# The first two tiles of the branch gate ga, projected ahead of the conv branch's output projection

## The chip, the cores and the metric

The kernel runs on one core of one Trainium2 chip, in one launch. The metric is the device time of one execution in microseconds, as the median of several runs.

## The reference, cut to what matters

One layer of a hybrid block over 512 latent tokens of 1024 features, with 256 context tokens ahead. The part around the change merges two branches:

```python
z = h @ w_in            # q, k, v, g, dd, cb, cc, ch, ga, gb are columns of z
y_gla = (o * silu(g)) @ w_gla_out            # o: normed heads of the gated linear attention
u = cc * ch
uc = seq_conv(u)        # width 3, within rows of 64 tokens
y_conv = (cb * uc) @ w_conv_out
merged = sigmoid(ga) * y_gla + sigmoid(gb) * y_conv
x = x + gt1 * (merged @ w_mix_out)
x = x + gt2 * swiglu(modulate(rmsnorm(x)))
```

The six modulation vectors (shift, scale and gate, twice) are `silu(c) @ w_ada + b_ada`.

## The kernel before

Everything is float32, computed as three products of exactly split halves (hi·hi, hi·lo, lo·hi): `mm3` (L148 to L151, all matmuls through L145). A weight comes in units of 512 KB into one of four raw buffers by a DMA from SyncE's queue (`raw_unit`, L118), ScalarE casts the high half `h_*` and VectorE subtracts the low half `l_*` (`split`, both recorded as L103); each half has four buffers. Two units make a slab of 256 columns (`Slab`), and `proj` multiplies it into two tiles of 128 features by 512 tokens: 24 matmuls of 128x512 for a tile, 48 for a pair. The tile accumulates in one of three PSUM banks that `proj` uses in turn (`bank`); the bank is free once the tile is read out.

Names in the rows leave numbers out, so `r_co`, `h_co`, `l_co` are the raw, high and low parts of the slabs of w_conv_out. In the order rows the numbers stand: `co0` is the slab of the first pair, `yc01` the second tile of pair 0.

After the attention the work runs in this order, pair by pair (four pairs of tiles each):

1. The short convolution (loop from L818): projections cc, ch and cb of a pair; VectorE makes `u`, then `uc`, then `cbu` = cb * uc (L845, which reads cb's bank out), and `split` makes `cuh` and `cul`, two of the eight parts of `cu`.
2. The conv branch's output (loop at L849): `yc`, a pair at a time, contracted over all eight parts of `cu`, in order; L854 multiplies the tile into `m` (the sigmoid of gb) and so reads the bank out.
3. The split of the attention's output `og` into `ogh` and `ogl`.
4. The loop at L862: a pair of `ga` tiles, ScalarE's sigmoid into `sa` (L869), then a pair of `yg` tiles, `yg * sa + m` (L876, L877) and the split into `me`.
5. The output projection `mx`, the residual, the second norm and SwiGLU.

Between these pairs `ada_tick` (L775) does the rest of the modulation in 16 steps, one at a call: it closes the last step with a small matmul `ad` of its sums (L781; L783 adds them to `gt`), loads two more units of w_ada (`r_wa`) and has VectorE fold them into `acc` with one operation and seven more (L805, L807), which are then cast and split as `accs`. The convolution loop calls it three times a pair, the loop of `yc` once a pair and the loop of `ga` once a pair, so the last four steps (`acc50` to `acc53`) are opened in the loop of `yc`.

What sets the order: outside the attention a scheduler orders each engine's instructions by when it reckons them ready. VectorE, ScalarE and SyncE's queue run them strictly in that order, so an instruction that waits holds all behind it.

Of the kernel before, what the change touches and what calls it, by code (L numbers as in the profile page):

```python
# [12 lines left out]
AF = mybir.ActivationFunctionType  # L13
# [18 lines left out]

# order of a head's attention on the tensor engine: its parts, and between them steps of other work
ORDER0 = "5 B 7 B 9 B 4 B 14 B 1 F0 5 B 1 kt0 1 A 4 F1 kv0 4 kt1 1 A 1 A 2 kv1 3 A 3 o 8 A 13 ot"
ORDER = "10 B 1 B 2 B 6 B 9 B 4 B F0 17 kt0 F1 A 2 kv0 2 kt1 11 kv1 A A 1 A A 2 o 33 ot"
ORDER3 = "3 B 4 B 3 B 12 B 4 B B 9 F1 F0 11 kt0 5 kv0 2 kt1 11 kv1 13 o 10 ot"

# columns of w_in
CQ, CK, CV, CG, CD = 0, 512, 1024, 2048, 3072
CCB, CCC, CCH, CGA, CGB = 3104, 4128, 5152, 6176, 7200  # L40

# rows of the small-vector tile
R_GM, R_GF, R_BA, R_GH, R_BD, R_WC, R_N = 0, 8, 16, 64, 66, 74, 98
# [3 lines left out]
def hybrid_block(ctx: ExitStack, tc: tile.TileContext, x, c, ctxt, c_ctx, w_ada, b_ada, g_mix, w_in,  # L47
# [45 lines left out]
    def pin(ins):  # L93
        """keeps the order on an engine as written, while a head's attention runs"""
        if pinned[0]:
            tc.keep_in_program_order(ins)
# [16 lines left out]

    # ---- weights: raw rows in, exact split into two parts of the tensor engine's width
    def raw_unit(src, name):
# [12 lines left out]
    class Slab:  # L128
        """Columns of a weight with 1024 rows (or k0..k1 tiles of rows), in units of at most 4 KiB per partition."""

# [24 lines left out]
    def rstd_of(ss, n, width, name):  # L155
        """(ss / width + EPS) ** -0.5 of n columns"""
        r = sm.tile([P, n], F32, tag=f"rs{n}", name=f"rs_{name}")
        act_.activation(r, ss, AF.Sqrt, bias=eps, scale=1.0 / width)
        dve.reciprocal(r, r)
        return r  # L160

    # ---- constants; the conditions first
    c_rows = cst.tile([16, P], F32, name="c_rows")
# [26 lines left out]
    for d in range(2):  # L190
        m = u2(f"m{d}")
        if d == 0:
            nc.vector.memset(m[:, P:2 * P], 1.0)
            nc.vector.tensor_copy(ones, m[:, P:2 * P])
        s = 1 if d == 0 else -1
        nc.gpsimd.memset(m, 1.0)
        # keep where s * (i - j) >= 0
        nc.gpsimd.affine_select(out=m[:, :P], in_=m[:, :P], compare_op=ALU.is_ge, fill=0.0, base=0,
                                pattern=[[s, P]], channel_multiplier=-s)
        mk = cst.tile([P, NT, P], U8, name=f"mask{d}")  # L200
        for s_ in range(NT):
            nc.vector.tensor_copy(mk[:, s_, :], m[:, :P])
        masks.append(mk)
# [10 lines left out]
    c2v = c2.rearrange("p (s k) -> p k s", s=2)  # L214
    # both parts of the conditions as four columns; their sum by pairs
    c4 = cst.tile([P, KT, 4], F32R, name="c4")
# [4 lines left out]

    # ---- small vectors, as columns
    vrow = u2("vrow")
# [11 lines left out]

    # ---- head: norm and transpose of the tokens; shift and scale of the first norm
    hp = tc.alloc_tile_pool(name="hp", bufs=1)
# [54 lines left out]
    def modulate(f):  # L292
        n = 4 if f in ADA_SPLIT else 2
        rsb = sm.tile([4, 256], F32, tag="adar", name=f"adar{f}", bufs=2)
        nc.vector.tensor_copy(rsb[0:n, :], rows[f][0:n, :256])
        cp = gbank(f"adac{f}")
        for s_ in range(2):
            nc.tensor.matmul(cp[:, 2 * s_:2 * s_ + 2], rsb[0:n, s_ * P:(s_ + 1) * P], sel[0:n, :], start=True, stop=True)
        nc.vector.tensor_tensor(modT[:, f], cp[:, 0:4].rearrange("p (s c) -> p s c", s=2),
                                vec[:, R_BA + f:R_BA + f + KT + 1:KT].unsqueeze(2).broadcast_to([P, 2, 2]), ALU.add)  # L300
        # g * (1 + scale)
        nc.vector.scalar_tensor_tensor(gs[:, f, :], modT[:, f, 1, :], 1.0,
                                       vec[:, R_GM + f:R_GM + f + 1].broadcast_to([P, 2]), ALU.add, ALU.mult)
        mod_split(xsT, f, 0, *h[f])
# [32 lines left out]
    def proj(slab, j, name, rhs=None, lo=0, n=T, o=None):  # L337
        """one tile of 128 output features by tokens"""
        o = bank(name) if o is None else o
# [4 lines left out]
    def proj_steps(slab, j, o, rhs=None, lo=0, n=T):  # L344
        """yields before each step of the contraction but the first"""
        rhs = rhs or h
# [9 lines left out]

    # ---- projections of a head, in parts: v by tokens, k and q by features
    pr = [dict(v=[None] * (NC_ + NT)) for _ in range(H)]
# [3 lines left out]
    def v_slab(hd):  # L362
        """the first head's slab carries the decay's low-rank columns too"""
        n = HV + 32
# [34 lines left out]
    def v_tile(hd, i):  # L399
# [13 lines left out]
        if hd == 0:  # L413
            # both parts of the decay's low rank, twice each
            st = stv[i // 4][:, i % 4, :].rearrange("p (d m l r) -> p d m l r", d=2, m=2, l=2)
# [33 lines left out]

    # the first head: latent tokens, while the context is normalised  # L450
    v_slab(0)
# [27 lines left out]
    def decays(hd):  # L479
        """log decays, summed within chunks"""  # L480
        t1s, las, bs = [], [], []
# [28 lines left out]
    def scaled(hd):  # L510
        """queries and keys times their decays, by features"""
        kT, qT = pr[hd]["kT"], pr[hd]["qT"]
# [48 lines left out]
    def scores(hd, d):  # L561
        q1, k1, q2, k2, ed, first_half, second_half = pr[hd]["parts"][d]
        # scores, transposed: [keys, queries] within pairs of chunks
        F = gbank(f"F{hd}{d}", (P, NT, P))
# [12 lines left out]
        dve.copy_predicated(TP[d], masks[d], F)  # L577
        # pairs of chunks as one step of the recurrence
        ed2 = ed.rearrange("p (s a) -> p s a", a=2)
# [12 lines left out]
    def keys(hd, d):  # L592
        """keys by tokens"""
        kt = gp.tile([P, NS - 1, P], F32R, tag="kt", name=f"kt{hd}{d}", bufs=2)
# [11 lines left out]
    def recur(hd, d):  # L606
        """states before each pair of the latent chunks"""
        v, kts, decs, states = (pr[hd][n] for n in ("v", "kts", "decs", "states"))
        S = None
        if d == 1:  # L610
            # both directions as one matrix
            pf = gp.tile([P, T], F32, tag="g2", name=f"pf{hd}", bufs=6)
# [46 lines left out]

    # ---- gates of the two branches, in parts  # L660
    mg = [None] * KT
# [16 lines left out]

    # weights of the work between the parts, in units of 512 rows by 256 columns: loaded four units ahead of their split
    G_ORDER = [("g", 0), ("g", 1), ("g", 2), ("gb", 0), ("gb", 1), ("g", 3), ("gb", 2), ("gb", 3)]  # L680
# [29 lines left out]
    def fills(hd):  # L710
        """steps of other work: the next head's projections, then gates"""
        if hd + 1 < H:
# [21 lines left out]
    work, nwork = None, 0  # L734
    # steps of other work at which the next unit of weights is split
    SPLITS = (3, 34, 60, 61)
# [31 lines left out]

    # ---- rest of adaLN: gates along tokens' rows, the second norm's shift and scale as columns
    mod2 = cst.tile([P, KT], F32, name="mod2")  # L770
# [4 lines left out]
    def ada_tick():  # L775
        """closes the last step of 256 columns, and opens another"""
        for m, q, acc in ada_open:
# [35 lines left out]

    # ---- short convolution
    ROWS, GW = T // CH, 64
    cu = []
    for pr in range(KT // 2):
# [24 lines left out]
        for j in range(2):  # L842
# [4 lines left out]
            split(t, hi, lo)  # L847
            cu.append((hi, lo))
    for pr in range(KT // 2):  # L849
        ada_tick()  # L850
# [11 lines left out]
    for pr in range(KT // 2):  # L862
        ada_tick()
        sl_ = Slab(w_in, CGA + pr * 256, 256, f"ga{pr}")
        sa = []
        for j in range(2):
            o = proj(sl_, j, f"ga{pr}{j}")
            t = ux(f"sa{pr}{j}")
            nc.scalar.activation(t, o, AF.Sigmoid)  # L869
            sa.append(t)  # L870
        sl_ = Slab(w_gla_out, pr * 256, 256, f"go{pr}")
        for j in range(2):
            i = 2 * pr + j
            o = proj(sl_, j, f"yg{pr}{j}", rhs=oghl)
            t = ux(f"yg{pr}{j}")
            nc.vector.tensor_mul(t, o, sa[j])  # L876
            nc.vector.tensor_add(t, t, mg[i])  # L877
            hi, lo = ux(f"meh{i}", F32R), ux(f"mel{i}", F32R)
            split(t, hi, lo)
            me.append((hi, lo))  # L880

    for i in range(2):
# [3 lines left out]

    # ---- output of the mixer, by tokens; residual; second norm
    x1 = []
# [71 lines left out]
    def steps_of(t):  # L960
        """other work within the last tokens' product, as its weights are let go"""
        if t < NT - 1:
# [19 lines left out]
    for t in range(NT):  # L982
# [9 lines left out]
        if t == 1:  # L992
            shift2(0)
    # ---- SwiGLU
    act = []
    for pr in range(FT // 2):
        if pr == 0:
            # the first tokens while the last are still being normalised
            todo = [(ff0["fa"], 0), (ff0["fa"], 1), (ff0["fb"], 0), (ff0["fb"], 1)]
# [27 lines left out]
    for ch in range(2):  # L1027
        sl_ = Slab(w_ffn_out, ch * 512, 512, f"fo{ch}", 0, FT)
        # the last tokens in halves, the first of them done while the second runs
        obs = [[((gbank if (t + ch) % 2 else bank)(f"fo{ch}{t}"), 0, 512, 0)] for t in range(NT - ch)]  # L1030
# [53 lines left out]
```

## Time and profile before

| | |
|---|---|
| median of 3 runs | 1029.73 us (1028.53 to 1031.1) |
| the profiled execution | span of 1028.8 us; no other time of it is given |
| TensorE | busy 1003.8 us, 98% of the span |
| VectorE | busy 548.6 us, 53% |
| ScalarE | busy 384.1 us, 37% |
| DMA | 117.16 MB, 114 GB/s in the mean |

The span is what the sum below is made against; it lies 0.9 us under the median of the runs. TensorE is busy nearly throughout, so the places to look at are those at which it waits or runs slowly.

### The profile page before, as it was taken

The page shows a single profiled execution, that of the slowest core. Times are in us where ns is not written, and L with a number is a line of the kernel's source. Part 1 is how long each engine was busy: PE and PEld are TensorE (multiplying, and loading weights), DVE is VectorE, ACT ScalarE, POOL GpSimd, SP SyncE. Part 2 cuts the span into 40 slices and gives each one's busy share as a digit, 9 for nine tenths or more (in the row PEclk, how much of TensorE's full clock was granted, in tenths as well). Part 3 has the DMA queues.
Part 4 walks back from the last instruction along what each step waited for, and adds up shares of the span by engine and source line. Part 5 has one row for each costly group of instructions (what it writes and reads, how often), then busy time and mean ns, then how long its engine had stood idle before and what let it go on. Part 6 is the DMA issues. An engine that isn't in the chain of part 4 may idle for free.

```text
span 1028.8 us, 13018 instructions
## 1 busy us (share of the span) xinstructions
PE 1003.8 (98%) x5270; PEld 833.0 (81%) x5274; DVE 548.6 (53%) x885; ACT 384.1 (37%) x594; POOL 6.2 (1%) x18
## 2 busy tenths in 40 slices
PE   6999999999999999998999999999999999999997
PEld 2598888888888888886888888898888888888886
DVE  4778776776535677769434434743343333322423
ACT  4556465557354222233123323552332232321323
POOL 2000000000000000000000000000000000000000
PEclk9999999999999999998999999999999999999999
DMA  8932211112336667566532322223233233232302
GB/s 248 273 111 63 61 29 55 42 41 66 101 104 186 187 191 220 164 207 212 146 100 82 103 103 82 82 86 119 82 100 105 82 103 102 83 124 80 123 22 82
DMA packets 117844, 117.16 MB, mean 114 GB/s; under 512 B 5414, under 2 KB 105880, under 8 KB 117784
## 3 DMA queue, kind: packets, MB, share of 16 engines
q1 hardware_dynamic: 117528, 116.07, 37.4%
q8 instruction: 41, 0.67, 0.3%
q0 software_dynamic: 256, 0.26, 0.1%
q14 instruction: 19, 0.16, 0.0%
HBM read 114.22 MB, written 2.10 MB: 113 GB/s over the span
## 4 chain that ended last, share of the span: by engine, by line
PE 75%; DVE 11%; DMA 9%; issue 2%; ACT 2%; SPq 1%; DVEq 0%; ACTq 0%
PE f L145 23%; PE fo L145 10%; DMA r_wa<-in_w_ada_dram 8%; PE v L145 5%; PE yg L145 4%; PE ga L145 4%; DVE acc L807 4%; PE yc L145 4%; PE g L145 4%; PE mx L145 3%; PE kl L145 2%; PE gb L145 2%; PE o L145 2%; PE F L145 2%; PE q L145 2%
## 5 line engine op out<-in xcount | busy, mean ns | idle before, releaser
L145 PE MATMUL f<-h,h_fa 128*128 128x512 f32 (+1 forms) x384 | 111.0, 373 | 0.2 <-DVE h L103 0.2
L145 PE MATMUL f<-h,h_fb 128*128 128x512 f32 (+1 forms) x384 | 110.2, 372 | 0.0
L145 PEld LDWEIGHTS f<-h,h_fa 128*128 128x128 f32 x384 | 70.2, 188 | 13.2 <-DVE h L103 0.8
L145 PEld LDWEIGHTS f<-h,h_fb 128*128 128x128 f32 x384 | 70.0, 188 | 12.4
L145 PE MATMUL f<-h,l_fb 128*128 128x512 f32 (+1 forms) x192 | 71.4, 372 | 0.0
L145 PE MATMUL f<-h,l_fa 128*128 128x512 f32 (+1 forms) x192 | 71.4, 372 | 0.0
L103 DVE TENSOR_TENSOR l_fa<-r_fa,h_fa 128x1024 fp32r<-128x1024 f32 x22 | 27.0, 1225 | 74.6 <-ACT h_fa L103 74.6
L103 DVE TENSOR_TENSOR l_fo<-r_fo,h_fo 128x1024 fp32r<-128x1024 f32 x22 | 26.9, 1225 | 68.7 <-ACT h_fo L103 68.7
L145 PE MATMUL fo<-h_fo,ah 128*128 128x512 f32 x154 | 60.6, 393 | 0.0
L145 PE MATMUL fo<-l_fo,ah 128*128 128x512 f32 x154 | 60.5, 393 | 0.0
L145 PE MATMUL fo<-h_fo,al 128*128 128x512 f32 x154 | 60.5, 393 | 0.0
L807 DVE SCALAR_TENSOR_TENSOR acc<-r_wa,c,acc 128x256 f32<-128x256 f32 x112 | 54.1, 483 | 5.2 <-DMA r_wa<-in_w_ada_dram 2.5
L145 PE MATMUL v<-h_v,h 128*128 128x256 f32 (+1 forms) x256 | 50.0, 289 | 1.9 <-DVE vl L103 1.7
L103 ACT CAST h_fo<-r_fo 128x1024 fp32r<-128x1024 f32 x22 | 23.1, 1050 | 71.0 <-PE fo L145 27.4
L145 PEld LDWEIGHTS v<-h_v,h 128*128 128x128 f32 x256 | 40.9, 191 | 2.8 <-DVE vl L103 1.9
L145 PEld LDWEIGHTS f<-h,l_fb 128*128 128x128 f32 x192 | 36.2, 188 | 6.2
L145 PEld LDWEIGHTS f<-h,l_fa 128*128 128x128 f32 x192 | 36.2, 188 | 6.3
L145 PE MATMUL g<-h,h_g 128*128 128x512 f32 x128 | 39.9, 393 | 0.0
L145 PE MATMUL gb<-h,h_gb 128*128 128x512 f32 x128 | 39.8, 392 | 0.0
L145 PE MATMUL cb<-h,h_cb 128*128 128x512 f32 x128 | 39.7, 392 | 0.0
L145 PE MATMUL ch<-h,h_ch 128*128 128x512 f32 x128 | 39.6, 391 | 0.0
L145 PE MATMUL cc<-h,h_cc 128*128 128x512 f32 x128 | 39.6, 391 | 0.0
(276 smaller groups left out, 2277.6 us busy)
## 6 DMA issues: line engine op xcount, KB each, us to landing
r_wa<-in_w_ada_dram SPq DMA_DIRECT2D x32, 512.0 KB, 4.7
r_fa<-in_w_ffn_in_dram SPq DMA_DIRECT2D x22, 512.0 KB
r_fb<-in_w_ffn_in_dram SPq DMA_DIRECT2D x22, 512.0 KB, 3.6
r_fo<-in_w_ffn_out_dram SPq DMA_DIRECT2D x22, 512.0 KB, 3.5
r_wa<-in_w_ada_dram SPq DMA_DIRECT2D x32, 256.0 KB, 4.1
r_kq<-in_w_in_dram SPq DMA_DIRECT2D x16, 256.0 KB, 4.4
r_g<-in_w_in_dram SPq DMA_DIRECT2D x8, 512.0 KB, 3.9
r_gb<-in_w_in_dram SPq DMA_DIRECT2D x8, 512.0 KB
```

The costliest lines, as they stand in the source:

```text
L103: return lambda *a, **k: pin(getattr(self.engine, op)(*a, **k))
L145: pin(nc.tensor.matmul(*a, **k))
L807: nc.vector.scalar_tensor_tensor(acc, w_[:, k, :], ck, acc, ALU.mult, ALU.add)
```

## The change

Pair 0 of `ga` is projected between the convolution and the loop of `yc`; the loop that held the `ga` pairs now does a `yg` pair and then the next `ga` pair. The sigmoids are kept in a table by pair and tile. Comments and docstrings are dropped as well, which issues nothing. Line numbers move with it: L854 of before is L865 of the changed kernel, L869 is L856, L876 is L880, L885 is L891 and L892 is L898.

```diff
             cu.append((hi, lo))
+    sas = {}
+
+    def branch_gate(pr):
+        sl_ = Slab(w_in, CGA + pr * 256, 256, f"ga{pr}")
+        for j in range(2):
+            o = proj(sl_, j, f"ga{pr}{j}")
+            sas[pr, j] = ux(f"sa{pr}{j}")
+            nc.scalar.activation(sas[pr, j], o, AF.Sigmoid)
+
+
+    branch_gate(0)
     for pr in range(KT // 2):
         ada_tick()
         sl_ = Slab(w_conv_out, pr * 256, 256, f"co{pr}")
...
     me = []
     for pr in range(KT // 2):
         ada_tick()
-        sl_ = Slab(w_in, CGA + pr * 256, 256, f"ga{pr}")
-        sa = []
-        for j in range(2):
-            o = proj(sl_, j, f"ga{pr}{j}")
-            t = ux(f"sa{pr}{j}")
-            nc.scalar.activation(t, o, AF.Sigmoid)
-            sa.append(t)
         sl_ = Slab(w_gla_out, pr * 256, 256, f"go{pr}")
         for j in range(2):
             i = 2 * pr + j
             o = proj(sl_, j, f"yg{pr}{j}", rhs=oghl)
             t = ux(f"yg{pr}{j}")
-            nc.vector.tensor_mul(t, o, sa[j])
+            nc.vector.tensor_mul(t, o, sas[pr, j])
             nc.vector.tensor_add(t, t, mg[i])
             hi, lo = ux(f"meh{i}", F32R), ux(f"mel{i}", F32R)
             split(t, hi, lo)
             me.append((hi, lo))
+        if pr + 1 < KT // 2:
+            branch_gate(pr + 1)
```

**TensorE, at the end of the convolution.** Before: the last `cb` tile (`cb31`), a closing `ad`, and the first `yc` tile.

```order
L145 MATMUL cb31_4365<-h1_133,h_cb3_4_4330 128x512
L145 MATMUL cb31_4365<-h3_135,h_cb3_4_4330 128x512
L145 MATMUL cb31_4365<-h1_133,l_cb3_4_4331 128x512
L781 MATMUL ad43_4396<-accs43_4319,ones_86 128x256 x2
L145 MATMUL yc00_4432<-cuh00_3547,h_co0_0_4422 128x512
L145 MATMUL yc00_4432<-cul00_3548,h_co0_0_4422 128x512
L145 MATMUL yc00_4432<-cuh00_3547,l_co0_0_4423 128x512
```

With the change, the same place:

```order
L145 MATMUL cb31_4365<-h1_133,h_cb3_4_4330 128x512
L145 MATMUL cb31_4365<-h3_135,h_cb3_4_4330 128x512
L145 MATMUL cb31_4365<-h1_133,l_cb3_4_4331 128x512
L145 MATMUL ga00_4408<-h0_132,h_ga0_0_4398 128x512
L145 MATMUL ga00_4408<-h2_134,h_ga0_0_4398 128x512
L145 MATMUL ga00_4408<-h0_132,l_ga0_0_4399 128x512
```

and 48 rows further, where the `ga` pair ends:

```order
L145 MATMUL ga01_4435<-h1_133,h_ga0_4_4404 128x512
L145 MATMUL ga01_4435<-h3_135,h_ga0_4_4404 128x512
L145 MATMUL ga01_4435<-h1_133,l_ga0_4_4405 128x512
L781 MATMUL ad43_4462<-accs43_4319,ones_86 128x256 x2
L145 MATMUL yc00_4498<-cuh00_3547,h_co0_0_4488 128x512
L145 MATMUL yc00_4498<-cul00_3548,h_co0_0_4488 128x512
L145 MATMUL yc00_4498<-cuh00_3547,l_co0_0_4489 128x512
```

The 48 matmuls of `ga00` and `ga01` have moved ahead of `ad43` and all `yc` tiles. It is the only move on TensorE: from the first `yg` tile on, its order is that of before.

**VectorE, between the last cu part and the read-out of the first yc tile.** Before (`cbu31` reads out the last `cb` tile, `cul31` is the last part of `cu`, `m00` reads out `yc00`):

```order
L845 TENSOR_TENSOR cbu31_4390<-cb31_4365,uc7_4298 128x512
L783 TENSOR_TENSOR gt41_4029<-gt41_4029,ad43_4396 128x256
L103 TENSOR_TENSOR l_co1_4_4513<-r_co1_4_4510,h_co1_4_4512 128x1024
L103 TENSOR_TENSOR cul31_4393<-cbu31_4390,cuh31_4392 128x512
L103 TENSOR_TENSOR accs52_4585<-acc52_4572,accs52_4585 128x256
L103 TENSOR_TENSOR ogl3_4749<-og11_2015,ogh3_4748 128x512
L805 TENSOR_SCALAR acc53_4656<-r_wa53_0_4657,c2_116 128x256
L103 TENSOR_TENSOR ogl4_4753<-og20_2549,ogh4_4752 128x512
L807 SCALAR_TENSOR_TENSOR acc53_4656<-r_wa53_0_4657,c2_116,acc53_4656 128x256
L103 TENSOR_TENSOR ogl5_4757<-og21_2551,ogh5_4756 128x512
L807 SCALAR_TENSOR_TENSOR acc53_4656<-r_wa53_0_4657,c2_116,acc53_4656 128x256
L854 TENSOR_TENSOR m00_2932<-yc00_4432,m00_2932 128x512
```

With the change `cul31` is followed by the whole step `acc52` and more. First the seven rows from `cul31` on:

```order
L103 TENSOR_TENSOR cul31_4393<-cbu31_4390,cuh31_4392 128x512
L805 TENSOR_SCALAR acc52_4638<-r_wa52_0_4639,c2_116 128x256
L807 SCALAR_TENSOR_TENSOR acc52_4638<-r_wa52_0_4639,c2_116,acc52_4638 128x256 x3
L807 SCALAR_TENSOR_TENSOR acc52_4638<-r_wa52_1_4645,c2_116,acc52_4638 128x256 x4
L103 TENSOR_TENSOR l_co1_0_4573<-r_co1_0_4570,h_co1_0_4572 128x1024
L783 TENSOR_TENSOR gt41_4029<-gt41_4029,ad43_4462 128x256
L891 SCALAR_TENSOR_TENSOR gt41_4029<-gt41_4029,gf1_5343 128x512
```

and the next ten, up to the read-out of `yc00`:

```order
L103 TENSOR_TENSOR l_co1_4_4579<-r_co1_4_4576,h_co1_4_4578 128x1024
L103 TENSOR_TENSOR accs52_4651<-acc52_4638,accs52_4651 128x256
L103 TENSOR_TENSOR ogl3_4815<-og11_2015,ogh3_4814 128x512
L805 TENSOR_SCALAR acc53_4722<-r_wa53_0_4723,c2_116 128x256
L103 TENSOR_TENSOR ogl4_4819<-og20_2549,ogh4_4818 128x512
L807 SCALAR_TENSOR_TENSOR acc53_4722<-r_wa53_0_4723,c2_116,acc53_4722 128x256
L103 TENSOR_TENSOR ogl5_4823<-og21_2551,ogh5_4822 128x512
L807 SCALAR_TENSOR_TENSOR acc53_4722<-r_wa53_0_4723,c2_116,acc53_4722 128x256
L103 TENSOR_TENSOR ogl6_4827<-og30_3142,ogh6_4826 128x512
L865 TENSOR_TENSOR m00_2932<-yc00_4498,m00_2932 128x512
```

Each step of w_ada stands one slab later than before: where `acc52` was done ahead of `cul31`, it now follows it, and `acc53` with its wait for `r_wa53` still stands ahead of `m00`.

**SyncE's queue, the loads ahead of acc53.** Before:

```order
L118 DMA r_co1_0_4504<-in_w_conv_out_dram 128x4x256
L118 DMA r_co1_4_4510<-in_w_conv_out_dram 128x4x256
L118 DMA r_wa52_0_4573<-in_w_ada_dram 128x4x256
L118 DMA r_wa52_1_4579<-in_w_ada_dram 128x4x256
L118 DMA r_co2_0_4588<-in_w_conv_out_dram 128x4x256
L118 DMA r_co2_4_4594<-in_w_conv_out_dram 128x4x256
L118 DMA r_wa53_0_4657<-in_w_ada_dram 128x4x256
L118 DMA r_wa53_1_4663<-in_w_ada_dram 128x4x256
```

With the change, where `r_co0` is issued at the place that `r_co1` had:

```order
L118 DMA r_co1_0_4570<-in_w_conv_out_dram 128x4x256
L118 DMA r_co1_4_4576<-in_w_conv_out_dram 128x4x256
L118 DMA r_wa52_0_4639<-in_w_ada_dram 128x4x256
L118 DMA r_wa52_1_4645<-in_w_ada_dram 128x4x256
L118 DMA r_co2_0_4654<-in_w_conv_out_dram 128x4x256
L118 DMA r_co2_4_4660<-in_w_conv_out_dram 128x4x256
L118 DMA r_wa53_0_4723<-in_w_ada_dram 128x4x256
L898 DMA x1_10_5350<-in_x_dram 128x512
L118 DMA r_wa53_1_4729<-in_w_ada_dram 128x4x256
```

The alternation of slabs and w_ada units is the same; `r_ga0` has gone in front of it, and a load of x now stands between the two units of `acc53`.

## Rows read from the trace of the kernel before

**Rows 1.** The page: the span, and busy time of each engine with its share.

```profile
span 1028.8 us, 13018 instructions
PE 1003.8 (98%) x5270; PEld 833.0 (81%) x5274; DVE 548.6 (53%) x885; ACT 384.1 (37%) x594; POOL 6.2 (1%) x18
```

**Rows 2.** Stretches: from:to, length, busy time of each engine, clock, DMA share, GB/s.

```profile
357.00:458.80 101.80, 101.80 (x463) 84.54 (x462) 76.37 (x138) 26.92 (x36) 0.00 (x0) 1.00 0.68 195
...
469.90:487.70 17.80, 14.60 (x52) 10.87 (x51) 15.67 (x30) 7.18 (x12) 0.00 (x0) 0.81 0.67 216
487.70:499.00 11.30, 11.30 (x51) 9.25 (x50) 6.12 (x9) 2.49 (x3) 0.00 (x0) 1.00 0.71 214
499.00:510.40 11.40, 11.40 (x51) 9.29 (x51) 4.07 (x5) 2.10 (x2) 0.00 (x0) 1.00 0.30 93
...
521.90:532.80 10.90, 10.90 (x51) 9.02 (x50) 3.38 (x4) 2.59 (x3) 0.00 (x0) 1.00 0.29 96
532.80:610.00 77.20, 77.20 (x338) 63.22 (x337) 31.16 (x35) 22.82 (x28) 0.00 (x0) 1.00 0.31 96
610.00:650.00 40.00, 40.00 (x178) 32.49 (x177) 20.38 (x30) 15.19 (x31) 0.00 (x0) 1.00 0.24 79
```

**Rows 3.** TensorE in order of time: start, duration, instruction, idle before it and releaser.

```profile
469.91 0.40 PE L781 MATMUL ad<-accs,ones 128*128 128x256 f32 x2
...
474.32 0.39 PE L145 MATMUL yc<-cuh,h_co 128*128 128x512 f32 x1
...
474.98 0.39 PE L145 MATMUL yc<-cuh,l_co 128*128 128x512 f32 x1
477.94 0.79 PE L145 MATMUL yc<-cuh,h_co 128*128 128x512 f32 x1 [2.58 <-ACT cuh L103]
479.36 0.79 PE L145 MATMUL yc<-cul,h_co 128*128 128x512 f32 x1 [0.62 <-DVE cul L103]
...
484.18 0.39 PE L145 MATMUL yc<-cuh,h_co 128*128 128x512 f32 x1
...
487.66 0.40 PE L781 MATMUL ad<-accs,ones 128*128 128x256 f32 x2
...
499.05 0.40 PE L781 MATMUL ad<-accs,ones 128*128 128x256 f32 x2
```

**Rows 4.** VectorE in order of time, around the end of the convolution.

```profile
470.94 1.53 DVE L807 SCALAR_TENSOR_TENSOR acc<-r_wa,c,acc 128x256 f32<-128x256 f32 x3
472.39 0.68 DVE L845 TENSOR_TENSOR cbu<-cb,uc 128x512 f32<-128x512 f32 x1
...
475.42 1.22 DVE L103 TENSOR_TENSOR l_co<-r_co,h_co 128x1024 fp32r<-128x1024 f32 x1
476.56 0.68 DVE L845 TENSOR_TENSOR cbu<-cb,uc 128x512 f32<-128x512 f32 x1
...
478.62 0.68 DVE L103 TENSOR_TENSOR cul<-cbu,cuh 128x512 fp32r<-128x512 f32 x1
...
481.54 0.35 DVE L805 TENSOR_SCALAR acc<-r_wa,c 128x256 f32<-128x256 f32 x1 [1.30 <-DMA r_wa<-in_w_ada_dram]
481.81 0.68 DVE L103 TENSOR_TENSOR ogl<-og,ogh 128x512 fp32r<-128x512 f32 x1
482.42 0.48 DVE L807 SCALAR_TENSOR_TENSOR acc<-r_wa,c,acc 128x256 f32<-128x256 f32 x1
...
483.81 0.68 DVE L854 TENSOR_TENSOR m<-yc,m 128x512 f32<-128x512 f32 x1
```

**Rows 5.** SyncE's queue: two issues of w_ada units, and issue to landing of nine.

```profile
476.67 2.43 SPq L118 DMA_DIRECT2D r_wa<-in_w_ada_dram x2
...
DMA to landing us min/median/max: 4.6/4.8/6.7
```

**Rows 6.** SyncE's queue, 400 to 700 us: its longest wait and its longest for a DMA.

```profile
SPq L118 <- DVE l_fa L103: 47.1, 6, 19.6
...
SPq L118 <- DMA r_wa<-in_w_ada_dram: 16.7, 6, 5.0
```

## The prediction

> **What bounds the kernel.** Read first the page's busy time of the engines: TensorE is busy 1003.8 of 1028.8 us, VectorE 548.6 [rows 1]. So only time in which TensorE waits or runs slowly can be had. Then the stretches around the edit: from the convolution (357 us) to 650 us TensorE is busy in all of each one at a granted clock of 1.00, its 2.4 GHz, but for one, 469.9 to 487.7, where it is busy 14.60 of 17.80 us at a clock of 0.81 [rows 2]. That stretch is the first pair of yc tiles. The same 48 matmuls and one ad take 487.66 to 499.05, 11.39 us, for the second pair; the first took 469.91 to 487.66, 17.75 us [rows 3]. **The first pair costs 17.75 - 11.39 = 6.4 us too much**, and that is all that can be gained here.
>
> TensorE in order of time shows its parts [rows 3]. At the usual distance of 11.15 / 48 = 0.232 us from matmul to matmul (11.39 less 0.24 for the ad):
> - 474.32 to 474.98 is two distances, 0.66 in place of 0.46: 0.2 us.
> - 474.98 to 477.94, one distance: 2.96 - 0.23 = 2.7 us, ended by ScalarE's cuh.
> - 477.94 to 479.36, one distance: 1.42 - 0.23 = 1.2 us, ended by VectorE's cul.
> - 479.36 to 484.18 is 11 distances, 4.82 - 2.55 = 2.3 us. Nothing is waited for here: the matmuls run 0.43 us apart, at the lower of the two clock levels (1.2 GHz), and get the higher one back at 484.
>
> Sum: 6.4 us. The cause is in VectorE's order [rows 4]. The contraction of yc runs over the eight parts of cu and wants the last one 21 matmuls after its start. The cb tiles end at 469.9, but VectorE, which works its order off strictly, reads the last one out at 476.56 and has its low half only at 478.62 + 0.68 = 479.3. Ahead of it stood a wait for the w_ada unit of acc52, its eight operations, and the low halves of co1. So the engine that bounds the kernel waits for one that is half idle, because of the order alone.
>
> **The change, part by part.**
>
> *The ga pair in front of yc.* It issues what it issued before: 48 matmuls, two slab units on SyncE's queue, two casts, two subtractions, two sigmoids. It needs only the normed tokens h and its slab, both long there: its units take the places that co0's had in the order of VectorE, and TensorE began co0 at 469.91 without a wait [rows 3]. A ga pair takes 10.9 us [rows 2], so it runs to 480.8, and yc00, behind the ad, starts at 481.05. Cost: nothing, since the same 10.9 us fall away behind yc.
>
> *What VectorE has done by then.* Up to cul31 its order is that of before, with ga0 and co0 in the places of co0 and co1, and acc50 and acc51 in those of acc51 and acc52; the loads go out behind the same releases. So I keep its times: cul31 is there at 479.3. The last part of cu is wanted at 481.05 + 21 x 0.232 = 485.9, 6.6 us later. Both waits and the slow clock behind them go: **-6.4 us**. If the part were late all the same, each us of it would cost one.
>
> *The banks.* Three banks go round. ga01, from 469.91 + 5.45 = 475.4, takes the bank of the last cb tile but one, whose read-out ends at 472.39 + 0.68 = 473.1; yc00 (481.05) takes that of the last one, read by 476.56 + 0.68 = 477.2 [rows 4]. Slack 2.3 and 3.8 us.
>
> *What is late next.* acc52 now stands behind cul31 and acc53 behind that, and behind acc53's first half stands m00, the read-out of yc00, whose bank yc11 wants. yc01 starts at 486.6, the second ad at 480.8 + 11.39 = 492.2, and yc11 at 492.2 + 0.24 + 5.58 = 498.0. For m00: the units of acc52 are issued where those of acc53 were, 476.67 and some 2 us later [rows 5]; the first operation then comes at 481.54 as there [rows 4]. Four operations take 0.35 + 1.53 = 1.9 us, to 483.4; the second unit lands at 478.7 + 4.8 = 483.5, and four more at 0.51 (1.53 / 3) end at 485.5. Then comes l_co1_0, at 475.42 to 476.56 a step of 1.14 us: 486.7. That frees a raw buffer for the load of acc53, which lands 4.8 us later, 491.5. The five operations between (l_co1_4, 1.14, and four of at most 0.61, the step of an ogl from 481.81 to 482.42) end by 490.3, so the load decides. From acc53's first operation to m00 took 481.54 to 483.81, 2.27 us, and has one ogl more now: 491.5 + 2.27 + 0.61 + 0.68 = 495.1. Slack 2.9 us. Price: none, while that holds. Above it, each us late is a us of TensorE, and a pause long enough brings the slow clock back, at most 2.3 us by the row. With both loads at their longest, 6.7 in place of 4.8 [rows 5], m00 ends at 498.9, 0.9 late: a cost of at most 0.9 + 2.3 = 3.2 us.
>
> A rule stands against this place. The trace first: through the whole convolution the same three banks go round, each waiting for VectorE's read-out, and TensorE is busy 101.80 of 101.80 us at a clock of 1.00 [rows 2]. The Trainium skill, TensorE: Matmul & The Clock Gate, section "A second HAM failure mode: psum-queue depth-cycling", says that cycling through PSUM banks makes TensorE pause between groups of matmuls often enough that its clock swings between the two levels. By the row the sum stays at -6.4; by the rule, were it to hold here, each swing would give back up to 2.3 us.
>
> *Behind yc.* yg follows yc directly, without ga between. Its inputs ogh and ogl are split during yc, m is read out in the first pairs' time, and sa is there since before yc; the go slab takes the place that ga0 had. TensorE's order from yg on is that of before, in a part where it never waited until 650 us [rows 2]. So the gain is carried to the end, if the loads move along with it: SyncE's long waits there are for VectorE letting a buffer go, 47.1 us in 6, its longest for a DMA is 16.7 in 6, w_ada's and so over by then [rows 6]. Nothing is priced for it.
>
> **Sum.** 1028.8 - 6.4 = 1022.4 us for the profiled span. The median of the runs lies 0.9 above that span: 1029.73 - 6.4 = **1023.4 us** (0.6%).
>
> **The rivals.**
> - *The slow clock stays.* The waits go, 4.1 us, but the 2.3 us at 1.2 GHz had another cause. For: nothing I see. Against: the clock is 1.00 in every neighbouring stretch and fell right after the pauses. 1029.7 - 4.1 = 1025.6.
> - *m00 is somewhat late.* Loads near their longest; yc11 waits for its bank and up to 3.2 us come back: 1023.4 to 1026.6. For: acc53 and the x load in front of its second half stand in m00's way, and two landings must both go as reckoned. Against: 2.9 us of slack.
> - *Slower: the wait moves to the banks and repeats.* m00 and m01 (behind acc53's second half) hold up yc11 and yc20 as long as cu held up yc00, with the slow clock after each: 2 x 6.4 - 6.4 gives 1029.7 + 6.4 = 1036.1. It loses from the point at which both together cost over 6.4; for one alone to wait the 3.9 us of the old pauses, m00 must be 2.9 + 3.9 = 6.8 us later than reckoned, so its load some 11.6 us under way. Against: the longest is 6.7 [rows 5].
> - *No difference: the time is given back.* A later stage, SwiGLU's first slabs say, is set by loads that do not move, and TensorE waits there for what it saved: 1029.7. Against: the DMA share is 0.24 from 610 to 650 us and the queue waits for buffers [rows 2, 6].
>
> That the change doesn't do what it says I give no chance: the order shows the 48 matmuls ahead of yc and no other move on TensorE.
>
> **How the numbers follow.** The whole gain 0.75, the slow clock stays 0.07, m00 late 0.10, given back 0.05, slower 0.03. About 0.3%, 3.1 us, is what a measurement of this kernel can tell from no change. The whole gain is faster by over that; of the clock's case (a gain of 4.1) 0.05, of m00's (3.2 to 6.4) 0.08. Faster 0.88; slower 0.03; the rest, 0.09, is the same. The forecast is 1023.4. Single runs lie up to 1.4 from their median; with 0.4 for the reading of the pauses the low end is 1021.6. The high end takes in the slow clock's case and m00's at its worst, 1026.6.
>
> **What would show it.** In the changed profile: no idle time of TensorE at the first yc tile, one clock of 1.00 from 460 to 520 us, the eight yc tiles at one pace, cul ending before yc starts, the span 6.4 us shorter with the pieces behind yg as long as before. Wrong would be: a wait of ga or yc for VectorE of over a us, at yc11's first matmul above all (m00); a stretch with 0.43 us between matmuls without a pause ahead; or a gain here that a wait behind 600 us takes back.

## The result and the profile after

| | before | with the change |
|---|---|---|
| first comparison, median | 1030.30 us (1028.53 to 1032.01, 5 runs) | 1024.88 us (1024.04 to 1025.91, 5 runs) |
| its ratio, 95% interval | | 0.9947 (0.9933 to 0.9960) |
| second comparison, median | 1031.77 us (1030.24 to 1033.73, 15 runs) | 1024.36 us (1023.71 to 1024.54, 5 runs) |
| its ratio, 95% interval | | 0.9924 (0.9911 to 0.9936) |
| span of the profiled execution | 1028.8 us | 1024.2 us |
| first cc to first mx matmul | 274.6 us | 268.2 us |

The kernel became faster by half to three quarters of a per cent. The last row is the sharpest: from the start of the convolution to the start of the output projection the gain is 274.6 - 268.2 = 6.4 us, the sum of the prediction. Its rows give for each tile the durations in ns (shortest, median, longest) and the first and last start in us; first of the kernel before, cc and mx:

```profile
L145 PE MATMUL cc<-h,h_cc x128: 387/389/487, 335.5 to 447.2; 128*128 128x512 f32 x128
L145 PE MATMUL mx<-h_mx,meh x64: 390/393/477, 610.1 to 655.8; 128*128 128x512 f32 x64
```

and mx with the change, whose cc row follows with the experiments (337.2):

```profile
L145 PE MATMUL mx<-h_mx,meh x64: 390/393/477, 605.4 to 651.1; 128*128 128x512 f32 x64
```

From the first mx matmul to the end it is 418.7 us before and 418.8 with the change. The profiled span fell by 4.6 only, and the stretches ahead of the convolution hold the rest.

The stretches of the kernel with the change, to be read beside [rows 2] (from:to, length, busy time of PE, PEld, DVE, ACT, POOL, clock, DMA share, GB/s):

```profile
358.70:460.50 101.80, 101.80 (x463) 84.51 (x462) 77.80 (x140) 26.94 (x35) 0.00 (x0) 1.00 0.68 194
471.50:482.50 11.00, 11.00 (x50) 9.10 (x49) 8.12 (x14) 3.33 (x4) 0.00 (x0) 1.00 0.64 202
482.50:493.90 11.40, 11.40 (x52) 9.29 (x51) 10.13 (x18) 5.49 (x9) 0.00 (x0) 1.00 0.88 275
493.90:505.30 11.40, 11.40 (x52) 9.29 (x51) 4.82 (x8) 2.41 (x4) 0.00 (x0) 1.00 0.52 176
534.00:611.00 77.00, 77.00 (x337) 62.97 (x336) 33.03 (x38) 22.94 (x28) 0.00 (x0) 1.00 0.30 95
611.00:645.00 34.00, 34.00 (x152) 27.66 (x151) 17.10 (x25) 13.35 (x29) 0.00 (x0) 1.00 0.20 65
```

The stretch that read 14.60 of 17.80 at a clock of 0.81 is gone: the ga pair, then every yc pair, is busy throughout at 1.00. TensorE in order of time shows the first two yc pairs at one length, 482.51 to 493.89 (11.38 us) and on to 505.29 (11.40), where [rows 3] had 17.75 and 11.39:

```profile
482.51 0.40 PE L781 MATMUL ad<-accs,ones 128*128 128x256 f32 x2
482.75 0.39 PE L145 MATMUL yc<-cuh,h_co 128*128 128x512 f32 x1
...
493.89 0.40 PE L781 MATMUL ad<-accs,ones 128*128 128x256 f32 x2
...
505.29 0.40 PE L781 MATMUL ad<-accs,ones 128*128 128x256 f32 x2
```

VectorE in order of time, against [rows 4]:

```profile
472.31 0.68 DVE L845 TENSOR_TENSOR cbu<-cb,uc 128x512 f32<-128x512 f32 x1
472.91 1.22 DVE L103 TENSOR_TENSOR l_co<-r_co,h_co 128x1024 fp32r<-128x1024 f32 x1
474.04 0.68 DVE L103 TENSOR_TENSOR cul<-cbu,cuh 128x512 fp32r<-128x512 f32 x1
476.97 0.35 DVE L805 TENSOR_SCALAR acc<-r_wa,c 128x256 f32<-128x256 f32 x1 [2.24 <-DMA r_wa<-in_w_ada_dram]
...
486.89 0.35 DVE L805 TENSOR_SCALAR acc<-r_wa,c 128x256 f32<-128x256 f32 x1 [0.72 <-DMA r_wa<-in_w_ada_dram]
...
489.75 0.69 DVE L865 TENSOR_TENSOR m<-yc,m 128x512 f32<-128x512 f32 x1
```

Here is the surprise. All of this trace runs 1.7 us later than the one of before (first cc matmul 337.2 against 335.5). On the time of before, the last cu part is done at 474.72 - 1.7 = 473.0, not at the 479.3 that the prediction kept, and m00 starts at 488.1, not at 494.4. VectorE was 6.3 us ahead of its old times. So two things changed at once: ga covers 10.9 us, and VectorE is earlier by 6.3. Without any cover yc, from 470.15, wants that part at 475.0, 2.0 us after it is there. Either alone might do.

### The profile page after: what moved, and what is told of

It reads as the page before. It is cut to its first block, busy times and chain, and to the rows that moved or that the text cites. A ratio compares the mean times of both kernels' runs of the same rounds, so it can differ in the third digit from the quotient of the medians.

```text
span 1024.2 us, 13014 instructions
## 1 busy us (share of the span) xinstructions
PE 1003.4 (98%) x5270; PEld 833.4 (81%) x5274; DVE 549.2 (54%) x885; ACT 384.2 (38%) x594; POOL 6.2 (1%) x18
## 4 chain that ended last, share of the span: by engine, by line
PE 92%; DVE 2%; ACT 2%; DMA 1%; issue 1%; SPq 0%; ACTq 0%
PE f L145 23%; PE fo L145 10%; PE v L145 5%; PE yc L145 4%; PE yg L145 4%; PE cb L145 4%; PE g L145 4%; PE ch L145 4%; PE cc L145 4%; PE gb L145 4%; PE ga L145 4%; PE mx L145 3%; PE kl L145 2%; PE o L145 2%; PE F L145 2%; PE q L145 2%
```

## The experiments

### What the time does by itself: the kernel of before and the changed kernel, once more

Edit: none in either.

> The kernel of before, unchanged, to see how far its own time and its opening stage (to the first cc matmul, 335.5 us in the trace of before, 337.2 in that of the change) move from run to run. Theory N (the opening differs by chance): ratio 1.000 within 0.2%, and a first cc matmul anywhere from 334 to 338 us. Theory O (the change makes the opening 1 to 2 us longer): the first cc matmul stays within 0.5 us of 335.5.

> The changed kernel once more. Its trace lost 6.4 us between the first cc and the first mx matmul, as reckoned, but the median moved by 5.4. Theory N: the ratio comes out nearer 0.9938 (6.4 us), and the first cc matmul lies in the same band as in the kernel of before. Theory O: the ratio stays at 0.9947 or above (at most 5.4 us), and the first cc matmul lies 1 to 2 us later than in the kernel of before.

Measured: before against itself 0.9997 (0.9984 to 1.0009), its own runs from 1027.64 to 1033.81; the change 0.9924 (0.9911 to 0.9936). The first cc matmul of the changed kernel, from the row of that tile in the first trace and in the second:

```profile
L145 PE MATMUL cc<-h,h_cc x128: 387/389/486, 337.2 to 448.9; 128*128 128x512 f32 x128
```

```profile
L145 PE MATMUL cc<-h,h_cc x128: 387/389/486, 335.7 to 447.4; 128*128 128x512 f32 x128
```

In the second trace of before it is at 336.5. So the opening is as early or late in either kernel (335.5 and 336.5 before, 337.2 and 335.7 after), as theory N has it, and what the first trace lost there belongs to the run. One thing that differs in the first 70 us is the granted clock, in the order of before, the first and the second trace of the change:

```profile
0.00:70.00 70.00, 58.70 (x357) 39.39 (x358) 48.16 (x138) 35.04 (x58) 6.17 (x18) 1.00 0.77 225
```

```profile
0.00:70.00 70.00, 59.76 (x346) 39.97 (x347) 46.70 (x133) 34.09 (x57) 6.17 (x18) 0.95 0.77 225
```

```profile
0.00:70.00 70.00, 60.35 (x356) 41.00 (x357) 48.14 (x137) 34.67 (x58) 6.17 (x18) 0.98 0.77 225
```

TensorE is not busy throughout there, and the granted clock of this stretch was 1.00, 0.95 and 0.98; the lowest is that of the run with the latest convolution. It alone was low from 30 to 70 us too, at 0.96, where the seven other traces of this text have 1.00. But this clock does not order the starts: the second trace of before, at 1.00, began cc at 336.5, and the three experiments at 0.98 at 335.4 to 336.2. So it is not shown that the clock accounts for the late start, and what brought it down in that run was not tried.

The part of theory N on the second ratio holds in direction only: 0.9924 is below the 0.9938 that was expected. The two intervals overlap from 0.9933 to 0.9936, 6.6 to 6.9 us. Two things in the runs go with the larger gain. The sets of runs of kernels in which yc still waits (before, and the kernel with less folding below) scatter by 3.5 to 6.2 us, those of the kernels in which it does not by 0.8 to 1.9. And the 15 runs of before in the second comparison had mean granted clocks of 0.993 to 0.996, with a median of 0.994, while its two profiled executions had 0.996 and 0.997. So most of these runs spent more time at the lower clock than the profiled ones; where they did, no trace shows.

### The w_ada steps one slab later, ga where it was

```diff
     for pr in range(KT // 2):
-        ada_tick()
+        if pr:
+            ada_tick()
         sl_ = Slab(w_conv_out, pr * 256, 256, f"co{pr}")
```

> The kernel of before with its ga pairs where they were, but without the w_ada step of the first yc pair, so that each of the last four steps is one slab later, as in the change. Theory C (the ga pair covers the wait, VectorE is as late as before, cul31 at 479): the first yc pair still takes 17.7 us and the time is that of before, ratio 1.000. Theory V (one w_ada step less ahead lets VectorE reach the last cu part about 6 us earlier, near 473 on the time of before, where yc wants it at 475.0): the first yc pair takes about 11.4 us with no wait over 0.3 us, ratio 0.994, with ga where it was.

Measured: 1024.38 us, ratio 0.9926 (0.9914 to 0.9939), the whole gain without moving ga. TensorE from the last cb matmul on, with no wait, the closing ad behind the first yc pair, and the stretch of that pair:

```profile
469.58 0.39 PE L145 MATMUL cb<-h,l_cb 128*128 128x512 f32 x1
469.80 0.40 PE L145 MATMUL yc<-cuh,h_co 128*128 128x512 f32 x1
...
481.00 0.40 PE L781 MATMUL ad<-accs,ones 128*128 128x256 f32 x2
```

```profile
469.60:481.00 11.40, 11.40 (x51) 9.18 (x50) 9.85 (x18) 5.56 (x9) 0.00 (x0) 1.00 0.75 235
```

VectorE ahead of the last cu part:

```profile
452.76 0.35 DVE L805 TENSOR_SCALAR acc<-r_wa,c 128x256 f32<-128x256 f32 x1 [2.52 <-DMA r_wa<-in_w_ada_dram]
464.13 0.35 DVE L805 TENSOR_SCALAR acc<-r_wa,c 128x256 f32<-128x256 f32 x1 [0.20 <-DMA r_wa<-in_w_ada_dram]
...
470.80 0.68 DVE L845 TENSOR_TENSOR cbu<-cb,uc 128x512 f32<-128x512 f32 x1
472.54 0.68 DVE L103 TENSOR_TENSOR cul<-cbu,cuh 128x512 fp32r<-128x512 f32 x1
```

The part is done at 473.2, wanted at 469.80 + 21 x 0.232 = 474.7. Theory V's 473 is met, theory C alone would have left 17.7 us for the pair; it took 481.00 - 469.80 = 11.20, with no ad in front of it. So moving the w_ada steps one slab later is enough by itself.

### ga ahead, with VectorE as late as before

```diff
+    ada_tick()
     branch_gate(0)
```

> The change, with the w_ada step of the first yc pair opened ahead of the ga pair instead of behind it, so that VectorE has the work ahead of the last cu part that it had before. Theory C: cul31 about 479 on the time of before, wanted at 485.9: no wait, the first yc pair takes 11.4 us, ratio 0.994. If only the later steps mattered (theory V without C), the first yc pair would wait as before and the ratio were 1.000. If each alone is enough, both this run and the one with the later steps alone show 0.994.

Measured: 1025.18 us, ratio 0.9933 (0.9919 to 0.9946). VectorE is as late as in the kernel of before (by 1.3 us later even, with the first cc matmul at 335.5 in both); the last row is m00:

```profile
477.85 0.68 DVE L845 TENSOR_TENSOR cbu<-cb,uc 128x512 f32<-128x512 f32 x1
479.91 0.69 DVE L103 TENSOR_TENSOR cul<-cbu,cuh 128x512 fp32r<-128x512 f32 x1
482.65 0.36 DVE L805 TENSOR_SCALAR acc<-r_wa,c 128x256 f32<-128x256 f32 x1 [1.11 <-DMA r_wa<-in_w_ada_dram]
492.57 0.68 DVE L866 TENSOR_TENSOR m<-yc,m 128x512 f32<-128x512 f32 x1
```

The last part is done at 480.6, yc starts at 481.2 and wants it at 486.1: no wait, and the pair takes 11.4 us:

```profile
470.00:481.00 11.00, 11.00 (x51) 9.12 (x50) 9.88 (x19) 4.95 (x7) 0.00 (x0) 1.00 0.59 191
481.00:492.40 11.40, 11.40 (x52) 9.29 (x51) 9.98 (x18) 5.52 (x9) 0.00 (x0) 1.00 0.80 239
```

This is the mechanism of the prediction by itself, with its own times. Each of the two is enough alone, and together they bring nothing more. In this kernel m00 ends at 493.3; yc11 wants its bank at 492.39 + 0.24 + 5.58 = 498.2. Even here 5.0 us were left.

### Half the cover

```diff
-    def branch_gate(pr):
-        sl_ = Slab(w_in, CGA + pr * 256, 256, f"ga{pr}")
-        for j in range(2):
-            o = proj(sl_, j, f"ga{pr}{j}")
+    def branch_gate(pr, js=(0, 1)):
+        w = 256 // (3 - len(js))
+        c0 = CGA + pr * 256 + js[0] * P
+        sl_ = Slab(w_in, c0, w, f"ga{pr}{js[0]}")
+        for j in js:
+            o = proj(sl_, j - js[0], f"ga{pr}{j}")
...
-    branch_gate(0)
+    ada_tick()
+    branch_gate(0, (0,))
...
         ada_tick()
+        if pr == 0:
+            branch_gate(0, (1,))
         sl_ = Slab(w_gla_out, pr * 256, 256, f"go{pr}")
```

> Only the first ga tile (24 matmuls, its own slab of 128 columns) stands ahead of the yc tiles, the second at the old place; the w_ada steps stand as in the kernel of before, so that VectorE is late as there. Theory C with its sum: the last cu part is done at about 480.6 on the time of before (as in the run with the whole pair ahead) and wanted at 470.1 + 5.45 + 0.24 + 4.87 = 480.7: a wait of under 0.5 us, the first yc pair takes 11.4 to 11.9 us, ratio 0.993 to 0.994. If the cover needs the whole pair (theory P: what counts is that the slab of co0 is split later, not the time), the first yc pair waits 2 us or more.

Measured: 1024.55 us, ratio 0.9941 (0.9923 to 0.9959); the first yc pair, 476.0 to 487.4, takes 11.4 us at a clock of 1.00:

```profile
476.00:487.40 11.40, 11.40 (x52) 9.30 (x51) 11.26 (x23) 5.68 (x10) 0.00 (x0) 1.00 0.81 249
```

One tile suffices, against theory P. It is not the edge that the sum had: the last cu part came at 478.02 + 0.68 = 478.7 and yc wanted it at 476.20 + 4.87 = 481.1. The first cc matmul is at 335.9 here, so on the time of before the part came at 478.3, 2.3 us earlier than reckoned. The slab of 128 columns is one unit instead of two, and VectorE's last two waits for w_ada's units ahead of the part were 0.99 us and none, against 3.13 and 0.94 in the run with the whole pair ahead; which of the two made it earlier was not tried. Without any cover the part would by the sum still have been 3.3 us late (wanted at 475.0).

### Less folding ahead of the last cu part

```diff
                 if z + k == 0:
                     nc.vector.tensor_scalar_mul(acc, w_[:, k, :], ck)
-                else:
+                elif (m, q) != (5, 2) or k == 0:
                     nc.vector.scalar_tensor_tensor(acc, w_[:, k, :], ck, acc, ALU.mult, ALU.add)
```

> The kernel of before with six of the eight VectorE operations of the w_ada step acc52 left out (that quarter of the last gate is then incomplete); its two loads stay. Theory W (VectorE's work ahead of the last cu part sets its time): 6 x 0.5 = 3.0 us less, the last cu part at 476.5 to 477.5 in place of 479.3 to 480.6, wanted at 475.0: the first yc pair still waits 1.5 to 2.5 us and takes 13 to 15.5 us, according to whether the clock falls after so short a pause; time 2 to 4.5 us under before. Theory L (the landing of the w_ada units sets it): the first yc pair takes 17.7 us as before.

Measured: 1028.16 us, ratio 0.9981 (0.9967 to 0.9995), 0.5 to 3.4 us faster, 2.9 by the medians. TensorE in order of time:

```profile
470.58 0.40 PE L781 MATMUL ad<-accs,ones 128*128 128x256 f32 x2
...
476.45 0.50 PE L145 MATMUL yc<-cuh,h_co 128*128 128x512 f32 x1 [0.60 <-ACT cuh L103]
477.87 0.50 PE L145 MATMUL yc<-cul,h_co 128*128 128x512 f32 x1 [0.92 <-DVE cul L103]
...
484.00 0.40 PE L781 MATMUL ad<-accs,ones 128*128 128x256 f32 x2
```

and the stretch of that pair:

```profile
470.60:484.00 13.40, 11.89 (x51) 9.18 (x50) 10.86 (x20) 7.10 (x11) 0.00 (x0) 1.00 0.77 235
```

The first pair takes 13.42 us, 2.0 more than 11.39 and 4.3 less than in before. So VectorE's work ahead of the last part counts, theory W, at the lower end of its range; theory L by itself would have left 17.7 us. But the landing of the units has a share. With the six operations gone, VectorE waited for the second unit of acc52, where it had not waited before:

```profile
470.61 0.35 DVE L805 TENSOR_SCALAR acc<-r_wa,c 128x256 f32<-128x256 f32 x1 [0.61 <-DMA r_wa<-in_w_ada_dram]
470.88 0.68 DVE L845 TENSOR_TENSOR cbu<-cb,uc 128x512 f32<-128x512 f32 x1
472.92 0.48 DVE L807 SCALAR_TENSOR_TENSOR acc<-r_wa,c,acc 128x256 f32<-128x256 f32 x1 [1.36 <-DMA r_wa<-in_w_ada_dram]
...
477.13 0.69 DVE L103 TENSOR_TENSOR cul<-cbu,cuh 128x512 fp32r<-128x512 f32 x1
```

From acc52's first operation to the end of the last part it is 7.2 us here and 479.3 - 470.55 = 8.8 in before: of 3.0 us of work left out, 1.5 came off. Here the clock stayed at 1.00: after pauses of 0.60 and 0.92 us no slow stretch followed.

## Why the prediction was right, and where not

- **The loss and its size.** Right. The first yc pair cost 6.4 us too much; the same piece of program is 6.4 us shorter in the trace after, and every yc pair takes 11.4.
- **Its parts.** Borne out: the slow clock belonged to the pause. It was gone with it in four kernels, and with the shorter pauses of the run with less folding only the waiting, 2.0 us, was left. The rival that the clock stays slow is out.
- **The cause.** Right: VectorE's order. Leaving out 3 us of its work took about half of the waiting away, 4.1 to 2.0 us, and all of the slow clock; having one w_ada step less ahead took all of both. What stood ahead was work and the landing of w_ada's units in turn, not work alone.
- **ga covers it.** Right as a mechanism: with VectorE as late as before it covers the wait alone, with 5.5 us to spare; 6.6 was reckoned. (21 matmuls is the distance to the part's high half; the low half is wanted one later, 0.23 us more room.) But it was not the whole of what the change does. That the total came out as reckoned says nothing for this step: with VectorE 6.3 us earlier the wait goes without ga too, so the same 6.4 us would have come out had the cover been wrong. Here the forecast had luck; only the two runs in which VectorE stays late show the cover.
- **"What VectorE has done by then."** Wrong. The prediction saw that acc50 and acc51 take the places of acc51 and acc52, and kept the old times, since "the loads go out behind the same releases". The first of these releases was itself earlier. Before, VectorE waited 4.79 us for the first unit of acc50 and folded it for 4 us, and cb3's low halves, whose end frees a raw buffer, stood behind that:

```profile
448.57 0.35 DVE L805 TENSOR_SCALAR acc<-r_wa,c 128x256 f32<-128x256 f32 x1 [4.79 <-DMA r_wa<-in_w_ada_dram]
448.96 3.61 DVE L807 SCALAR_TENSOR_TENSOR acc<-r_wa,c,acc 128x256 f32<-128x256 f32 x7
452.49 1.22 DVE L103 TENSOR_TENSOR l_cb<-r_cb,h_cb 128x1024 fp32r<-128x1024 f32 x1
```

With the change acc50 no longer stands there, and the first of the low halves came at 447.69 - 1.7 = 446.0 on the time of before, 6.5 us earlier:

```profile
447.69 1.22 DVE L103 TENSOR_TENSOR l_cb<-r_cb,h_cb 128x1024 fp32r<-128x1024 f32 x1 [1.93 <-ACT h_cb L103]
```

The next unit of w_ada went out as that half ended, at 448.94 - 1.7 = 447.2; before, the unit at that place went out at 453.73. The four pairs of loads behind it (slab, w_ada, slab, w_ada) moved by 6.3 to 6.8 us, and cul31 ended up 6.3 us earlier. The rows:

```profile
448.94 0.37 SPq L118 DMA_DIRECT2D r_wa<-in_w_ada_dram x1
```

with the change, and before:

```profile
453.73 0.37 SPq L118 DMA_DIRECT2D r_wa<-in_w_ada_dram x1
```

- **What is late next.** The slack of 2.9 us at m00 was mis-sized for the same reason: m00 ended at 490.4, yc11 wanted its bank at 493.89 + 0.24 + 5.58 = 499.7, so 9.3. With VectorE as late as before it was 5.0. The rivals that hung on it (m00 late, the wait moved to the banks) had less room than they were given. The yc pairs take the three banks in turn with TensorE busy 11.40 of 11.40 us at a clock of 1.00. So the rule of the Trainium skill, TensorE: Matmul & The Clock Gate, section "A second HAM failure mode: psum-queue depth-cycling", that pauses between groups of matmuls come with such cycling and make the clock swing, is not borne out at this place.
- **Carried to the end.** Right: behind yc TensorE is busy throughout, 77.00 of 77.00 us, and the gain at the first mx matmul (274.6 to 268.2) is there in full; behind it the two traces are as long as each other, 418.7 and 418.8 us, so nothing was given back.
- **The total.** 1024.88 lies in the range; the 1.5 us to the forecast are of the size by which the openings of the two traces of the changed kernel differed (337.2 and 335.7). That the openings make up the difference is not shown, since only one execution of each comparison is profiled.

## What to carry to other kernels

Before costing a cover, ask what stands ahead of the late operand on the engine that makes it: here one step of background work less ahead of it, the last four steps each one slab later, brought the whole gain without moving ga. When an edit shifts work on a strictly ordered engine, replay it from the first place at which the orders differ: buffers, loads and releases downstream all move with that place. And a wait on the bounding engine can cost more than its idle time (3.2 us idle, 6.4 us in all, of which 2.3 at the lower clock), so compare equal pieces of work by their length instead of adding up idle rows.

## What the hardware showed that was not expected

Two short pauses cost only themselves in the one trace that has them: with idle times of 0.60 and 0.92 us the clock of the stretch stayed at 1.00, whereas with 2.58 and 0.62 us in the kernel of before it read 0.81 over the pair, and 0.90 in its second trace, with 0.36, 2.56 and 0.92 us:

```profile
470.90:488.60 17.70, 13.86 (x52) 10.24 (x51) 15.41 (x30) 7.16 (x11) 0.00 (x0) 0.90 0.66 209
```

The pair took 17.7 us in both of these, since the second trace lost less to the clock (1.7 us against 2.3) and more to waiting (4.7 against 4.1). And the opening 70 us, where TensorE waits for loads and for VectorE, ran at clocks of 0.95 to 1.00 in executions with the same instructions there, and two executions of the one changed kernel began the convolution 1.5 us apart.
